# A decoder layer with sparse attention: subtractions shared out between VectorE and GpSimd, a written lookahead for each piece, and a new TensorE order

## The chip, the cores and the metric

The kernel runs on one core of a Trainium2 chip. The metric is the device time of one execution in microseconds. A core has TensorE (PE in the rows; its weight loads are PEld), VectorE (DVE), ScalarE (ACT), GpSimd (POOL) and SyncE (SP), which here only issues transfers. Each engine takes its instructions strictly in the order of its own queue.

## The reference

One layer over 512 positions of width 1024. The input is projected once; the columns go to three groups of mixers (causal pooling, a short gated convolution, and sparse attention with a compressed, a selected and a sliding branch), each with a SiLU gate; the groups' outputs are concatenated, projected, added to the scaled input and normalised.

```python
proj = x @ w_in
y_pool = jax.nn.silu(pool_z) * pool_mixer(pool_v, pool_w, pool_scale)
y_conv = jax.nn.silu(conv_z) * short_conv_mixer(conv_b, conv_c, conv_x, conv_w)
y_nsa = jax.nn.silu(nsa_z) * nsa_mixer(q, k_cmp, v_cmp, k_slc, v_slc, k_win, v_win, gates, ...)
y = jnp.concatenate([y_pool, y_conv, y_nsa], axis=-1) @ w_out
return layer_norm(ALPHA * x + y, ln_g, ln_b)
```

With 512 positions every block of keys is among the selected, so the selected and the sliding branch both attend to all earlier positions, with their own keys and values.

## The kernel before

**Split products.** TensorE multiplies in a rounded 32-bit form (fp32r). To keep precision, an operand is split into a rounded part and a rest: ScalarE writes the rounded part (`cast`, L79), and `rest` (L86) subtracts it from the original. A product then takes three matmuls. Line 86 is therefore one line for many subtractions: of weights (`hl<-raw,hl`, always on VectorE), of the turned attention weights (`ptl<-Y,pth`, always on GpSimd), of the gated outputs (`yln<-yo,yhn`) and others.

**Pieces and their order.** TensorE's instructions stand in the order in which the program writes them (`mm`, L67). The string `ORDER` (L26) writes it: each letter runs one step of a generator. `f` is the next piece of projection work: 12 matmuls with half of a chunk of 128 output columns, for which `weights` loads 256 KB, casts and subtracts; or a piece of the compression; or one of the eight first halves of the output projection. `s` scores a pair of heads against all keys of one branch (`scores`, L245): two matmuls into an `S` bank per head, VectorE adds the bias and takes the row's extreme (L257), ScalarE the exponential (L259). After that `scale` (L433) multiplies by the gate and the reciprocal of the sum (the gate product is L438, 128x2 or 128x4), and `turn` transposes through VectorE (L450) and a round trip to DRAM into `Y`. `v` (`values`, L459) splits `Y` into `pth` and `ptl` and multiplies with the values into an `O` bank. `c` scores the compressed keys (`cmp_scores`), `e` closes a query block of a head group (`finish`, L480): one matmul into its `O` bank, then for each of two halves a copy by ScalarE (L491) and an addition by VectorE (L492), then the product with the gate `zn` (L493) and the split. `o` is a piece of `second_part` (L644), which completes the output projection of 128 positions and normalises them.

**Banks.** Two `pj` banks take chunks, four `S` banks scores and small products, two `O` banks the attention outputs. A query block of a head group holds an `O` bank from its first `v` to the end of its `finish`; the blocks come in the order 3, 1, 0, 2 (`QB_ORDER`), first for one head group and then for the other. The third block therefore takes the bank of the first: its first `v` (the seventh of all) waits for the first `finish`.

**The other engines.** Their instructions are ordered by a planner, which simulates the engines and takes, among what is ready on an engine, the instruction with the highest priority. Earlier in the program is higher, and `tc.high_priority(offset=n)` moves what stands in it n places ahead. Before the change the offsets are one number per kind of work: weights 60 (`PRI_W`), compression 100 (`PRI_C`), normalisation 10 and 60 at the end, and 0 for scores, values, gates and finishes. The evacuation of the compression's input (`xs`, L332) and of queries has none. The planner's order is fixed when the program is built.

**The end.** `second_part` normalises each of four blocks: per half a sum of residual and product with its row sum (L664), a mean (L666), a square with its sum on ScalarE (L668), then small steps to the variance (L676 to L680), a power on GpSimd (L681), and two passes per half (L690, L696) before the store. The last block's second half is cut in two quarters.

Of the kernel before, what the change touches and what calls it, by code (L numbers as in the profile page):

```python
# [28 lines left out]
PRI_F = 0  # L29
# [23 lines left out]
def hybrid_layer(ctx, tc, xT, xres, wk4, wv, wc, wo, w1k, w1v, small, poolw, relb, onehot, lng, lnb,  # L53
# [266 lines left out]
    def blocks(i, pe_col):  # L320
        XS = y_tile("xs").rearrange("p a b -> p (a b)").rearrange("p (c t s) -> p c t s", c=16, t=2)
        pec = small_t[:, pe_col:pe_col + 16]
        act.activation(XS[:, :, 0, 31], pec, AF.Copy)
        rest(dve, XS[:, :, 1, 31], pec, XS[:, :, 0, 31])
        dve.memset(XS[:, :, :, 63].bitcast(F32), 0.0)
        p = yield from chunk(2 + i)
        for g in range(2):
            for par in range(2):
                src = p[64 * g:64 * g + 64]
                src = bass.AP(tensor=src.tensor, offset=src.offset + par, ap=[src.ap[0], [2, 16], [16, 31]])  # L330
                d = slice(64 * par, 64 * par + 64)
                act.activation(XS[d, :, 0, g * 32:g * 32 + 31], src, AF.Copy)  # L332
                rest(dve, XS[d, :, 1, g * 32:g * 32 + 31], src, XS[d, :, 0, g * 32:g * 32 + 31])
        return XS

    def compress(i, w1, w2_col):
# [9 lines left out]
        with tc.high_priority(offset=PRI_C):  # L346
            hs = tmp("hs", 256)
            act.activation(hs, hp[:, :256], AF.Copy)  # L348
        yield
        with tc.high_priority(offset=PRI_C):  # L350
# [12 lines left out]
        with tc.high_priority(offset=PRI_C):  # L363
# [18 lines left out]
    def gate_of(z, p):  # L382
        with tc.high_priority(offset=PRI_E):
            act.activation(z, p, AF.Tanh, scale=0.5)
            dve.scalar_tensor_tensor(z, z, 1.0, p, op0=OP.add, op1=OP.mult)  # L385
# [47 lines left out]
    def scale(qb, g, c, brs, P, st):  # L433
# [4 lines left out]
        dve.tensor_tensor(sv, sv, gv[:, :, 1 + brs[0]:1 + brs[0] + nb], op=OP.mult)  # L438
# [20 lines left out]
    def values(qb, g, c, brs, Y):  # L459
# [6 lines left out]
        for k0 in range(0, nk, 2):  # L466
# [6 lines left out]
            rest(pool, tl, t, th)  # L473
# [6 lines left out]
    def finish(qb, g, th):  # L480
# [6 lines left out]
        with tc.high_priority(offset=PRI_F):  # L487
# [31 lines left out]
    def put_y(k, y):  # L519
        y_parts()  # L520
        act.activation(ypc["h"][:, k], y, AF.Copy)
        rest(dve, ypc["l"][:, k], y, ypc["h"][:, k])
# [85 lines left out]
    def wo_parts(half, k):  # L608
        if (half, k) in WO:
            return WO[half, k]  # L610
        if k in (4, 5):
            with tc.high_priority(offset=PRI_W):
# [18 lines left out]
    def first_part(half, tb):  # L631
# [8 lines left out]
        dve.scalar_tensor_tensor(r, r, ALPHA, o, op0=OP.mult, op1=OP.add)  # L640

    GB = []

    def second_part(tb, final):  # L644
# [12 lines left out]
        for i, (half, a, b) in enumerate(cuts):  # L657
# [5 lines left out]
            with tc.high_priority(offset=PRI_END if final else PRI_LN):  # L663
                dve.scalar_tensor_tensor(x, x, 1.0, o, op0=OP.mult, op1=OP.add, accum_out=m[:, i:i + 1])  # L664
                if i == 0:
                    dve.tensor_scalar(m[:, 6:7], m[:, 0:1], -1.0 / 512 / 32, None, op0=OP.mult)  # L666

                act.activation(o, x, AF.Square, bias=m[:, 6:7], scale=1.0 / 32, accum_out=m[:, 3 + i:4 + i])  # L668
                if i == n - 2:
# [12 lines left out]
        on_pool = [] if tb in QB_ORDER[LN_POOL:] else [i for i in range(2) if LN_PAT[i] == "p"]  # L682
        for i, (half, a, b) in enumerate(cuts):
            x = R[tb, half][:, a:b]
            with tc.issue_after(ready.ins):
                if i in on_pool:
                    pool.tensor_scalar(x, x, m[:, 7:8], m[:, 11:12], op0=OP.add, op1=OP.mult)
                    pool.tensor_tensor(x, x, GB[half], op=OP.mult)
                else:
                    dve.scalar_tensor_tensor(x, x, m[:, 7:8], GB[half][:, a:b], op0=OP.add, op1=OP.mult)  # L690
        for i, (half, a, b) in enumerate(cuts):
            x = R[tb, half][:, a:b]
            if i in on_pool:
                pool.tensor_tensor(x, x, GB[2 + half], op=OP.add)
            else:
                dve.scalar_tensor_tensor(x, x, m[:, 11:12], GB[2 + half][:, a:b], op0=OP.mult, op1=OP.add)  # L696
            (nc.scalar if final and i == 1 else nc.sync).dma_start(out[tb, :, half, a:b], x)
# [15 lines left out]
    def q_chunk(c):  # L713
        p = yield from chunk(c - 2)
        queries(c, p)
# [32 lines left out]
    def attend():  # L748
        for n, u in enumerate(subs):
            with tc.high_priority(offset=PRI_A):  # L750
# [3 lines left out]
    def weigh():  # L754

        while scored:
            n, u, P, st = scored.pop(0)
            with tc.high_priority(offset=PRI_A):
                scale(*u, P, st)
                turned.append((u, turn(n, P)))  # L760

    def gather():
        while True:
            (qb, g, c, brs), Y = turned.pop(0)
            with tc.high_priority(offset=PRI_V):
# [104 lines left out]
```

## Time and profile before

| what | value |
|---|---|
| median of 3 runs | 275.31 us (274.36 to 276.69) |
| the profiled execution | 275.69 us, of which the span from first to last instruction 273.9 us |
| TensorE matmul busy | 251.7 us, 92% of the span |
| VectorE busy | 216.0 us, 79% |
| ScalarE busy | 185.3 us, 68% |
| GpSimd busy | 91.0 us, 33% |
| mean granted TensorE clock | 0.971 |

Matmuls overlap each other in the records, so a row's duration is longer than the pace: 24 matmuls of 128x512 advance the chain by 5.46 us. What tells whether TensorE is held is the idle time before a row (in brackets in the timeline) and the granted clock of a stretch, in which 1.00 is the upper of its two levels, 2.4 GHz, and 0.50 the lower, 1.2 GHz.

### The profile page before, as it was taken

To read this page: it belongs to the slowest core of one execution; us is meant where nothing else is said; L and a number is where in the kernel's file an instruction comes from. 1 tells how busy PE (TensorE), PEld (TensorE's weight loads), DVE (VectorE), ACT (ScalarE), POOL (GpSimd) and SP (SyncE) were. 2 spreads that over 40 slices of the span, in tenths; PEclk is the share of its full clock that TensorE was granted. 3 is DMA by queue.
4 is the path that set the end of the run, shared out by engine and by line. 5 is a ranking of instruction groups with operands and counts; after the bars stand their busy time and mean duration, and the time that the engine had idled before them with its cause. 6 is when DMAs were issued, how large, how long until landed. Compare 5 with 4: busy or idle time off the path is not lost.

```text
span 273.9 us, 4510 instructions
## 1 busy us (share of the span) xinstructions
PE 251.7 (92%) x1241; PEld 208.8 (76%) x1241; DVE 216.0 (79%) x568; ACT 185.3 (68%) x441; POOL 91.0 (33%) x112
## 2 busy tenths in 40 slices
PE   8899999969997899939999799999999999999970
PEld 5677997757887788738888678878888888888760
DVE  2672948757998999999897989899669648795685
ACT  3763748658998997877668999996586336452330
POOL 4100800040043345243337452355342153104831
PEclk9999999999999999968999889999999999999995
DMA  6864963783579787674566387798565897520232
GB/s 209 308 191 126 194 200 111 257 203 120 169 233 241 245 234 217 219 225 174 166 203 171 134 250 201 250 265 266 173 187 199 270 304 203 150 76 21 94 117 78
DMA packets 38454, 52.42 MB, mean 191 GB/s; under 512 B 4691, under 2 KB 22780, under 8 KB 38396
## 3 DMA queue, kind: packets, MB, share of 16 engines
q1 hardware_dynamic: 37964, 51.93, 62.4%
q8 instruction: 10, 0.16, 0.3%
q10 hardware_dynamic: 464, 0.20, 0.3%
q14 instruction: 16, 0.13, 0.2%
HBM read 38.47 MB, written 14.04 MB: 192 GB/s over the span
## 4 chain that ended last, share of the span: by engine, by line
PE 59%; DVE 13%; issue 10%; DMA 6%; POOL 5%; ACT 3%; SPq 2%; DVEq 0%; POOLq 0%; ACTq 0%
PE bk L69 48%; PE o L69 5%; PE s L69 4%; DVE hl L86 3%; POOL ptl L86 3%; DMA small_t<-small 2%; DVE P L257 2%; DMA scrp<-X 2%; DVE X L450 2%; DMA Y<-scrp 2%; DVE r L696 1%; ACT hl L79 1%; DVE r L664 1%; ACT bk L668 1%; POOL ln L681 1%
## 5 line engine op out<-in xcount | busy, mean ns | idle before, releaser
L69 PE MATMUL bk<-xh,hl 128*128 128x512 f32 x384 | 125.4, 396 | 3.0 <-DVE zn L385 2.2
L86 POOL TENSOR_TENSOR ptl<-Y,pth 128x512 fp32r<-128x512 f32 (+1 forms) x44 | 54.3, 1245 | 104.5 <-ACT pth L79 102.5
L69 PEld LDWEIGHTS bk<-xh,hl 128*128 128x128 f32 x384 | 72.6, 190 | 20.6 <-DVE zn L385 2.6
L69 PE MATMUL bk<-xl,hl 128*128 128x512 f32 x192 | 75.7, 394 | 0.0
L86 DVE TENSOR_TENSOR hl<-raw,hl 128x512 fp32r<-128x512 f32 (+1 forms) x72 | 51.2, 717 | 19.5 <-ACT hl L79 19.0
L79 ACT ACTIVATE hl<-raw 128x512 fp32r<-128x512 f32 (+1 forms) x72 | 42.9, 604 | 24.2 <-PE bk L69 19.9
L69 PEld LDWEIGHTS bk<-xl,hl 128*128 128x128 f32 x192 | 36.5, 190 | 7.3 <-DVE xl L86 0.3
L259 ACT ACTIVATE P<-P,st 128x512 f32<-128x512 f32 (+3 forms) x64 | 35.3, 553 | 4.0 <-DVE st L257 3.5
L441 ACT ACTIVATE P<-P,st 128x512 f32<-128x512 f32 (+3 forms) x64 | 31.1, 552 | 3.0 <-DVE st L438 2.4
L257 DVE CUSTOM_DVE_ANT_0 P<-s,T 128x512 f32<-128x512 f32 (+3 forms) x64 | 28.6, 482 | 1.7 <-PE s L69 1.2
L79 ACT ACTIVATE pth<-Y 128x512 fp32r<-128x512 f32 (+1 forms) x44 | 24.5, 582 | 6.6 <-POOL ptl L86 2.6
L450 DVE STREAM_TRANSPOSE X<-P 128x512 f32<-128x512 f32 (+2 forms) x48 | 27.7, 605 | 0.6 <-ACT P L441 0.3
L69 PE MATMUL o<-pth,VS 128*128 128x256 f32 x80 | 21.6, 297 | 4.8 <-DVE yo L492 4.7
L69 PE MATMUL s<-KS,qs 128*128 128x512 f32 (+2 forms) x96 | 23.8, 371 | 1.6 <-ACT hs L348 0.8
L69 PE MATMUL o<-ptl,VS 128*128 128x256 f32 x80 | 21.7, 299 | 3.2 <-POOL ptl L86 3.1
L69 PEld LDWEIGHTS s<-KS,qs 128*128 128x128 f32 x96 | 16.8, 194 | 5.0 <-ACT hs L348 1.1
L69 PEld LDWEIGHTS o<-pth,VS 128*128 128x128 f32 x80 | 15.9, 199 | 6.0 <-issue 5.1
L69 PE MATMUL bk<-hl,yhp 128*128 128x512 f32 x64 | 20.2, 396 | 0.0
L69 PEld LDWEIGHTS o<-ptl,VS 128*128 128x128 f32 x80 | 16.0, 200 | 5.1 <-POOL ptl L86 4.4
L668 ACT ACTIVATE bk<-r,ln 128x512 f32<-128x512 f32 (+1 forms) x9 | 5.8, 640 | 16.5 <-DVE ln L666 12.9
L69 PEld LDWEIGHTS bk<-hl,yhp 128*128 128x128 f32 x64 | 11.8, 188 | 2.6
L69 PE MATMUL bk<-hl,ylp 128*128 128x512 f32 x32 | 12.7, 395 | 0.0
(167 smaller groups left out, 376.5 us busy)
## 6 DMA issues: line engine op xcount, KB each, us to landing
raw<-wc SPq DMA_DIRECT2D x40, 256.0 KB, 3.2
scrp<-X SPq DMA_DIRECT2D x12, 512.0 KB, 3.1
Y<-scrp SPq DMA_DIRECT2D x48, 128.0 KB, 4.3
raw<-wo SPq DMA_DIRECT2D x16, 256.0 KB, 2.9
scrp<-X SPq DMA_DIRECT2D x8, 384.0 KB, 3.0
Y<-scrp SPq DMA_DIRECT2D x32, 96.0 KB, 2.4
r<-xres SPq DMA_DIRECT2D x8, 256.0 KB, 5.1
out<-r SPq DMA_DIRECT2D x7, 256.0 KB, 2.0
```

Source lines behind the costliest of these rows:

```text
L69: return tc.keep_in_program_order(pe.matmul(*args, **kw))
L79: act.activation(dst, src, AF.Copy)
L86: eng.tensor_tensor(dst, src, h.bitcast(F32), op=OP.subtract)
L257: dve.tensor_tensor_reduce(out=P[:, j, b], in0=p[:, b], in1=T[:, h, 512 - w:], scale=-1.0, scalar=BIG, op0=OP.add, op1=OP.min, accum_out=s ...
L259: act.activation(P[:, j, b], P[:, j, b], AF.Exp, bias=st[:, 0, j, b:b + 1], scale=-1.0, accum_out=st[:, 1, j, b:b + 1])
L441: act.activation(P[:, j, b], P[:, j, b], AF.Copy, scale=st[:, 1, j, b:b + 1])
L450: dve.transpose(X[:, :, :, h].rearrange("p j k s -> p k j s"), P[:, h].rearrange("p b (k j s) -> p (b k) j s", j=4, s=32))
L664: dve.scalar_tensor_tensor(x, x, 1.0, o, op0=OP.mult, op1=OP.add, accum_out=m[:, i:i + 1])
L668: act.activation(o, x, AF.Square, bias=m[:, 6:7], scale=1.0 / 32, accum_out=m[:, 3 + i:4 + i])
L681: pool.tensor_tensor(m[:, 11:12], m[:, 10:11], mhalf, op=OP.pow)
L696: dve.scalar_tensor_tensor(x, x, m[:, 11:12], GB[2 + half][:, a:b], op0=OP.mult, op1=OP.add)
```

## The change

Three things are rewritten; what is computed stays the same.

1. `ENG` gives each single subtraction or product its engine. Of the 68 weight subtractions that `weights` makes, 30 go to GpSimd; of the 44 `ptl` subtractions, 18 go to VectorE; of the 24 gate products of L438, 9 go to GpSimd; of the 8 products with `zn`, 4; of the 8 subtractions of `yln`, 1.
2. `AHEAD` gives each piece of each kind its own offset, 20 times a digit, in place of one offset per kind. Kinds that had none (compressed scores `k`, queries `q`, `xs` `x`, the splits of `put_y` `y`, the additions of `first_part` `r`) get one, and scaling (`m`) and turning (`t`) get one each.
3. `ORDER` is a new string with the same letters. The first `s` stands after 3 letters `f` instead of 8, the first `e` ahead of the twelfth `s` instead of behind it, the second `e` ahead of the seventh `v`; the sixth `c`, the ninth `v` and others move by up to three letters `f`.

At the end, the third block's normalisation passes are issued behind the last block's first mean; of the last block, the first of the second half's quarters may be normalised as soon as its mean is known, and the stores of the first half and of that quarter swap their queues.

```diff
-ORDER = 'ffffffffssfffffffffssfffsvfffssfvfffvfcsfsvfcfffsvsfffsevcsvevffffvscfevffsfsfsvcvsevffsfssvffcvsfvefffvffvsfsvfcefvffffvfvcffvfeffvefooooooooo'
+ORDER = 'fffsfffffsfffffffffssffsfvfffsfvsffsfvfcfsvfcfffsvsfffesvcsevvfffvfscfveffsfsfsvcvsevffcsfvssffvsffvefffvsfvfesvvfcffffvffcffevfffvfveooooooooo'
+AHEAD = {
+    'c': '959549', 'f': '41096608', 'k': '11011402', 'm': '421690533210053042023000', 'q': '20', 'r': '84751010',
+    's': '401032580053839606633100', 't': '002048505000085633022423', 'v': '091035350020997197125450',
+    'w': '006142361099275378536090313980932105459923933500690630432363221843055577',
+    'x': '43240150', 'y': '0505', 'z': '36060004',
+}
+ENG = {
+    'g': 'vpvpvpvvpvpvpvvvvvvpvpvp',
+    't': 'vvppppvppvppppvpppvvppppppvppvvpppvvvpvvvvpv',
+    'w': 'pvpvpvppppppvvpvpvvvvpppppvvvpvpvvvvvpppvvvvvvvvvpvpvvpvpvpvvvvvpppp',
+    'y': 'ppvpvvpv', 'z': 'vvvvpvvv',
+}
...
+    def ahead(kind):
+        i = cnt["+" + kind] = cnt.get("+" + kind, -1) + 1
+        return tc.high_priority(offset=20 * int(AHEAD[kind][i]))
+    def turn_of(kind):
+        i = cnt[kind] = cnt.get(kind, -1) + 1
+        return eng[ENG[kind][i]]
     def weights(src, n):
-        with tc.high_priority(offset=PRI_W):
+        with ahead("w"):
...
-            parts(raw, hl[:, 0, :n], hl[:, 1, :n])
+            parts(raw, hl[:, 0, :n], hl[:, 1, :n], turn_of("w"))
...
-        dve.tensor_tensor(sv, sv, gv[:, :, 1 + brs[0]:1 + brs[0] + nb], op=OP.mult)
+        turn_of("g").tensor_tensor(sv, sv, gv[:, :, 1 + brs[0]:1 + brs[0] + nb], op=OP.mult)
...
-            rest(pool, tl, t, th)
+            rest(turn_of("t"), tl, t, th)
...
-        with tc.high_priority(offset=PRI_F):
+        with ahead("f"):
...
+            while late:
+                with tc.issue_after(first.ins):
+                    late.pop()()
...
+                with tc.issue_after(early if final and i == 1 else ready.ins):
...
-            (nc.scalar if final and i == 1 else nc.sync).dma_start(out[tb, :, half, a:b], x)
+                (nc.scalar if final and i == 0 else nc.sync).dma_start(out[tb, :, half, a:b], x)
+        if tb == QB_ORDER[-2]:
+            late.append(norm)
+        else:
+            norm()
```

## Rows read from the trace of the kernel before

**Rows 1.** The head of the profile's page: the span, and busy time, share of the span and instructions of each engine; and the first line of the chain of waits that ended last, in shares of the span.

```profile
span 273.9 us, 4510 instructions
...
PE 251.7 (92%) x1241; PEld 208.8 (76%) x1241; DVE 216.0 (79%) x568; ACT 185.3 (68%) x441; POOL 91.0 (33%) x112
...
PE 59%; DVE 13%; issue 10%; DMA 6%; POOL 5%; ACT 3%; SPq 2%; DVEq 0%; POOLq 0%; ACTq 0%
```

**Rows 2.** The table of stretches: start and end of a stretch in us, its length, the busy time of each engine in it with the number of instructions, the granted TensorE clock, the DMA engines' busy share and GB/s.

```profile
42.00:64.00 22.00, 19.60 (x92) 15.80 (x91) 14.31 (x33) 14.52 (x33) 2.78 (x3) 1.00 0.61 180
...
64.00:182.00 118.00, 108.11 (x541) 90.76 (x540) 109.92 (x330) 104.42 (x275) 45.24 (x52) 0.96 0.69 207
...
182.00:230.00 48.00, 48.00 (x237) 40.50 (x236) 36.45 (x81) 27.45 (x59) 17.80 (x18) 1.00 0.74 229
...
265.60:273.90 8.30, 0.00 (x0) 0.00 (x0) 4.46 (x15) 1.79 (x6) 0.99 (x1) 0.66 0.27 97
```

**Rows 3.** The timeline of TensorE: four of its waits. Columns: start us, duration us, engine, line, operation, out<-in, shape, count, and in brackets the idle time before it and what ended it.

```profile
56.99 0.50 PE L69 MATMUL bk<-xh,hl 128*128 128x512 f32 x1 [2.17 <-DVE zn L385]
...
93.28 0.61 PE L69 MATMUL s<-KS,qs 128*128 128x384 f32 x2 [0.75 <-ACT hs L348]
...
120.56 0.55 PE L69 MATMUL o<-pth,VS 128*128 128x256 f32 x1 [4.73 <-DVE yo L492]
...
155.16 0.39 PE L69 MATMUL o<-ptl,VS 128*128 128x256 f32 x1 [1.32 <-POOL ptl L86]
```

**Rows 4.** The table of stretches again, by two microseconds, behind the two waits that lower the clock.

```profile
120.00:122.00 2.00, 1.44 (x6) 1.38 (x7) 1.91 (x8) 0.62 (x2) 0.00 (x0) 0.50 0.65 188
...
122.00:124.00 2.00, 2.00 (x8) 1.81 (x7) 1.88 (x8) 1.98 (x5) 0.38 (x1) 0.50 0.33 101
...
124.00:126.00 2.00, 2.00 (x8) 1.54 (x8) 1.91 (x8) 1.95 (x5) 1.67 (x2) 0.76 0.38 148
...
128.00:130.00 2.00, 2.00 (x11) 1.64 (x10) 1.93 (x6) 0.93 (x3) 0.20 (x1) 1.00 0.77 260
...
156.00:158.00 2.00, 2.00 (x6) 1.61 (x7) 1.94 (x7) 2.00 (x7) 0.99 (x1) 0.50 0.41 131
...
158.00:160.00 2.00, 1.86 (x10) 1.55 (x9) 2.00 (x13) 1.86 (x6) 1.54 (x2) 0.73 1.01 253
```

**Rows 5.** The timeline from the first `finish` to the end of the longest wait (the last matmul into its bank, the copy and the addition of either half, and one small product between them), and the same four steps of the last `finish`.

```profile
113.14 0.39 PE L69 MATMUL o<-pct,VC 128*128 128x512 f32 x1
...
115.14 0.38 ACT L491 ACTIVATE yo<-o 64x256 f32<-64x256 f32 x1
...
116.18 0.41 DVE L492 TENSOR_TENSOR yo<-o,yo 64x256 f32<-64x256 f32 x1
...
117.78 0.38 ACT L491 ACTIVATE yo<-o 64x256 f32<-64x256 f32 x1
...
118.67 1.21 DVE L554 TENSOR_TENSOR edge<-edge,pv 64x16 f32<-64x16 f32 x1
...
119.98 0.43 DVE L492 TENSOR_TENSOR yo<-o,yo 64x256 f32<-64x256 f32 x1
...
240.09 0.38 ACT L491 ACTIVATE yo<-o 64x256 f32<-64x256 f32 x1 [1.29 <-PE o L69]
...
242.22 0.43 DVE L492 TENSOR_TENSOR yo<-o,yo 64x256 f32<-64x256 f32 x1
```

**Rows 6.** Groups of VectorE instructions between 64 and 182 us: line, engine, operation, out<-in, shape, count, busy us in all, mean ns of one, idle time before them.

```profile
L86 DVE TENSOR_TENSOR hl<-raw,hl 128x512 fp32r<-128x512 f32 x31 | 22.7, 736 | 3.0 <-ACT hl L79 3.0
...
L438 DVE TENSOR_TENSOR st<-st,G 128x2 f32<-128x2 f32 (+1 forms) x19 | 4.8, 251 | 0.3
...
L493 DVE TENSOR_TENSOR yo<-yo,zn 128x256 f32<-128x256 f32 x4 | 1.8, 459 | 0.0
```

**Rows 7.** Groups of GpSimd instructions over the whole span, in the same columns.

```profile
L86 POOL TENSOR_TENSOR ptl<-Y,pth 128x512 fp32r<-128x512 f32 (+1 forms) x44 | 54.3, 1245 | 104.5 <-ACT pth L79 102.5
...
L681 POOL TENSOR_TENSOR ln<-ln,mhalf 128x1 f32<-128x1 f32 x4 | 4.0, 996 | 22.5 <-DVE ln L680 22.5
...
L86 POOL TENSOR_TENSOR bdl<-bd,bdh 128x256 fp32r<-128x256 f32 x1 | 0.7, 742 | 0.1
...
L418 POOL TENSOR_TENSOR pc<-pc,cm 128x124 f32<-128x124 f32 (+3 forms) x8 | 2.6, 331 | 6.8 <-DVE cm L417 3.0 <-DMA raw<-wc 1.5 <-ACT P L441 1.2
```

**Rows 8.** The timeline where a weight subtraction of VectorE meets a subtraction of GpSimd, and one that meets none.

```profile
106.15 1.28 POOL L86 TENSOR_TENSOR ptl<-Y,pth 128x512 fp32r<-128x512 f32 x1 [0.69 <-DMA raw<-wc]
...
106.27 1.71 DVE L86 TENSOR_TENSOR hl<-raw,hl 128x512 fp32r<-128x512 f32 x1
...
112.11 0.69 DVE L86 TENSOR_TENSOR hl<-raw,hl 128x512 fp32r<-128x512 f32 x1 [0.16 <-ACT hl L79]
```

**Rows 9.** The timeline of the end: the third block's normalisation, the last block's first cut between, and the last block's own normalisation.

```profile
261.74 1.41 DVE L690 SCALAR_TENSOR_TENSOR r<-r,ln,lng 128x512 f32<-128x512 f32 x2
...
263.73 0.68 DVE L664 SCALAR_TENSOR_TENSOR r<-r,bk 128x512 f32<-128x512 f32 x1
...
264.33 0.75 DVE L696 SCALAR_TENSOR_TENSOR r<-r,ln,lnb 128x512 f32<-128x512 f32 x1
...
265.34 0.15 DVE L666 TENSOR_SCALAR ln<-ln 128x1 f32<-128x1 f32 x1
...
267.64 0.16 DVE L680 TENSOR_TENSOR ln<-ln 128x1 f32<-128x1 f32 x1
```

More of the change, by code (lines that the diff above doesn't have):

```diff
@@ L331, in blocks @@
                 d = slice(64 * par, 64 * par + 64)
-                act.activation(XS[d, :, 0, g * 32:g * 32 + 31], src, AF.Copy)
-                rest(dve, XS[d, :, 1, g * 32:g * 32 + 31], src, XS[d, :, 0, g * 32:g * 32 + 31])
+                with ahead("x"):
+                    act.activation(XS[d, :, 0, g * 32:g * 32 + 31], src, AF.Copy)
+                    rest(dve, XS[d, :, 1, g * 32:g * 32 + 31], src, XS[d, :, 0, g * 32:g * 32 + 31])
         return XS
@@ L345, in compress @@
                 mm(hp[:, :256], x[:, c], hl[:, :, j * 128:j * 128 + 128], start=c == 0, stop=c == 15)
-        with tc.high_priority(offset=PRI_C):
+        with ahead("c"):
             hs = tmp("hs", 256)
@@ L349, in compress @@
         yield
-        with tc.high_priority(offset=PRI_C):
+        with ahead("c"):
             hq = bank("S", "hq")
@@ L362, in compress @@
         yield
-        with tc.high_priority(offset=PRI_C):
+        with ahead("c"):
             o = bank("S", "cmpo")
@@ L382, in gate_of @@
     def gate_of(z, p):
-        with tc.high_priority(offset=PRI_E):
+        with ahead("z"):
             act.activation(z, p, AF.Tanh, scale=0.5)
@@ L520, in put_y @@
         y_parts()
-        act.activation(ypc["h"][:, k], y, AF.Copy)
-        rest(dve, ypc["l"][:, k], y, ypc["h"][:, k])
+        with ahead("y"):
+            act.activation(ypc["h"][:, k], y, AF.Copy)
+            rest(dve, ypc["l"][:, k], y, ypc["h"][:, k])
     mix_z = {}
@@ L611, in wo_parts @@
         if k in (4, 5):
-            with tc.high_priority(offset=PRI_W):
+            with ahead("w"):
                 raw, _ = load(wo[k, half], 512)
@@ L639, in first_part @@
         r = R[tb, half]
-        dve.scalar_tensor_tensor(r, r, ALPHA, o, op0=OP.mult, op1=OP.add)
+        with ahead("r"):
+            dve.scalar_tensor_tensor(r, r, ALPHA, o, op0=OP.mult, op1=OP.add)
     GB = []
+    late = []
     def second_part(tb, final):
@@ L665, in second_part @@
                 if i == 0:
-                    dve.tensor_scalar(m[:, 6:7], m[:, 0:1], -1.0 / 512 / 32, None, op0=OP.mult)
+                    first = dve.tensor_scalar(m[:, 6:7], m[:, 0:1], -1.0 / 512 / 32, None, op0=OP.mult)
                 act.activation(o, x, AF.Square, bias=m[:, 6:7], scale=1.0 / 32, accum_out=m[:, 3 + i:4 + i])
@@ L714, in q_chunk @@
         p = yield from chunk(c - 2)
-        queries(c, p)
+        with ahead("q"):
+            queries(c, p)
     def pieces(fs):
@@ L749, in attend @@
         for n, u in enumerate(subs):
-            with tc.high_priority(offset=PRI_A):
+            with ahead("s"):
                 scored.append((n, u, *scores(*u)))
@@ L757, in weigh @@
             n, u, P, st = scored.pop(0)
-            with tc.high_priority(offset=PRI_A):
+            with ahead("m"):
                 scale(*u, P, st)
+            with ahead("t"):
                 turned.append((u, turn(n, P)))
@@ L764, in gather @@
             (qb, g, c, brs), Y = turned.pop(0)
-            with tc.high_priority(offset=PRI_V):
+            with ahead("v"):
                 values(qb, g, c, brs, Y)
@@ L775, in compressed @@
             assert pcts[0] - pcts[1] < len(PCT)
-            pcs[qb, g] = cmp_scores(qb, g)
+            with ahead("k"):
+                pcs[qb, g] = cmp_scores(qb, g)
             yield
```

60 lines of the change are left out of this document (34 added, 26 removed).

## The prediction

> **What bounds the kernel now.** I read the busy shares first, then the chain of waits. TensorE is busy for 92% of the span and holds 59% of the chain [rows 1], so the time is TensorE's work plus the time in which it is held or slowed. Next, the table of stretches says where it is held. Nothing is lost from 182 us on until its work ends: 48.0 of 48 us [rows 2]. The last 8.3 us hold no matmul, only the end of the normalisation. Between 64 and 182 us it is busy for 108.1 of 118 us, so 9.9 us are waits; between 42 and 64 it lacks 2.4 us [rows 2].
>
> In the same 118 us VectorE is busy for 109.9 and ScalarE for 104.4 us, GpSimd for 45.2 [rows 2]. The reader should see three engines near their limit there and one with room: VectorE has 8.1 us of idle time, and whatever TensorE waits for stands in a full queue.
>
> Then the timeline of TensorE, for what ended its waits. The longest is 4.73 us before the seventh `v`, ended by an addition of `finish` on VectorE; next come 2.17 us before a chunk (`zn` evacuated late), 1.32 us for a subtraction on GpSimd, 0.75 us for a bank [rows 3]. Last, the granted clock: behind the longest wait TensorE runs at the lower level, 0.50 from 120 to 124 us and 0.76 on average from 124 to 126, where the same two microseconds hold 8 matmuls and not 11 [rows 4]. What it lost there is busy time times the missing share of the clock: 1.44 x 0.50 + 2.0 x 0.50 + 2.0 x 0.24 = 2.2 us. Behind the 1.32 us it is 2.0 x 0.50 + 1.86 x 0.27 = 1.5 us [rows 4]. At full clock the stretch's matmuls need 108.1 - 3.7 = 104.4 us.
>
> **The shares of the engines.** All terms are for 64 to 182 us, since VectorE has room elsewhere. By the start times of the weight subtractions the 19th to 48th of the string fall there; 10 of them leave VectorE: 10 x 0.736 = 7.4 us [rows 6]. Of the 44 turned-weight subtractions [rows 7] the 3rd to 30th fall there, 28, and 7 of these arrive; one of this shape that meets nothing takes 0.69 us on VectorE [rows 8], so 4.8 us. Six gate products leave, 6 x 0.251 = 1.5, and three `zn` products, 3 x 0.459 = 1.4 us [rows 6]. VectorE: 7.4 + 1.5 + 1.4 - 4.8 = 5.5 us less, 104.4 in place of 109.9. GpSimd: 3 more long subtractions at 1.28 us [rows 8], three products of 256 columns at 0.74, and six tiny products that it never did before: the nearest rows are 0.33 us for a product of up to 124 columns and 1.0 us for a power of one column [rows 7]; I take 0.33, as the same operation, and keep 1.0 for the range. In all 3.8 + 2.2 + 2.0 = 8 us more (12 at the other end), 53 of 118: not a bound by its sum. These 5.5 us are no gain in themselves. They are room.
>
> A rule speaks against moving subtractions to GpSimd. A weight subtraction that starts beside one of GpSimd takes 1.71 us, one that meets none 0.69 [rows 8]. GpSimd's own takes 1.28. So the two take turns, and a piece that is moved costs almost twice as long and may hold up its old engine. The Trainium skill (GPSIMD Engine Reference, Specifications and Engine selection) says that GpSimd's SBUF interface is shared with VectorE, against instructions with two SBUF inputs, and that elementwise work belongs on VectorE since GpSimd is about twice as slow with two inputs; by that rule the moves lose. These rows agree with it for the single instruction. In the sum I take few collisions, for the 31 weight subtractions of the stretch now average 0.736 us beside 28 of GpSimd's [rows 6]: (0.736 - 0.69) x 31 = 1.4 us in all. The rest is a rival.
>
> **The longest wait.** The first `finish` issues its matmul at 113.14; its four steps start at 115.14, 116.18, 117.78 and 119.98 and end at 120.41, although they take only 0.38 + 0.41 + 0.38 + 0.43 = 1.6 us [rows 5]. Between them VectorE does scores and a 64x16 product that takes 1.21 us beside GpSimd. The last `finish`, among less work, needs 2.6 us from 240.09 to 242.65 [rows 5]. The change does two things to it. The first digit of `f` puts it 80 places ahead (0 before), and the matmul is issued ahead of the twelfth `s`. Until the seventh `v`, TensorE then has the 2.7 us that it has now (113.14 to 115.83), the twelfth `s` (four matmuls of 384 columns, 0.68 us at the pace of 0.2275 us for 512) and the second `e` (0.23): 3.6 us. The chain needs 0.39 for the matmul, 1.6 for the steps, and before each of four steps about half of a running 0.69 us instruction, 1.4: 3.4 us. It just fits; since the thirteenth `s` has a lead of 160 and can still push in, I keep 0.7 us. Gain 4.73 - 0.7 = 4.0 us (bounds 0 and 4.73). The 2.2 us of clock stand behind this wait and go with it (bounds 0 and 2.2). What is late next is the wait for `S` banks around it.
>
> **The chunk's wait.** At 56.99 TensorE has waited 2.17 us for a bank that `zn` or `xs` holds [rows 3]. GpSimd is busy 2.8 of the 22 us there [rows 2], and four of the six weight subtractions of these chunks go to it, 2.8 us off VectorE; `xs` gets leads of 20 to 80 places and `zn` 60. I take 1.4 us, two thirds, as the transfers of the turned weights crowd this stretch too; bounds 0 and 2.17.
>
> **The end.** The last block's first addition (L664) starts at 263.73, behind 1.41 us of the third block's passes from 261.74; its mean comes at 265.34 only, with another pass (0.75 us from 264.33) between [rows 9]. The change puts these passes behind that mean, and one quarter's pass into the wait before L680 at 267.64. VectorE's work in the last 10 us stays the same, and it is nearly full there, so only its small holes go: 0.5 us (bounds 0 and 1.0). The swapped store queues move one issue between two queues that both end with a store anyway; 0.
>
> **The rest.** The first `s` stands earlier: it only moves the two bias steps and exponentials of one score ahead of 42 us, where no wait is at stake; 0. The other waits of the stretch (9.9 - 4.73 = 5.2 us, with 1.5 us of clock) have no single cause that the change takes away: I leave them, bounds -4 and +6. Against that stand pieces that now come earlier, the ninth `v` by one `f` and the sixth `c` by three, and weights with a lead of 0: one new wait of the size of the present smaller ones, +1.0 us.
>
> **Sum.** The profiled execution took 275.69 us, 0.4 over the median of 275.31 and inside the runs' spread. -4.0 - 2.2 - 1.4 - 0.5 + 1.0 = -7.1, so 268.6; I say 268.5.
>
> **Rivals.** (1) The waits only move: the planner works from its own picture of the engines, and VectorE, ScalarE and TensorE all need 104.4 us of the 118, so what one piece gains by a lead another loses. For it: every offset is relative, and nearly all rise. Against it: one wait is worth 6.9 us with its clock, and its cover grows by arithmetic. New waits of 6 us eat the gain: 274.5. Chance 0.18.
>
> (2) Slower, by collisions: of the 31 long GpSimd subtractions then in the stretch (28 - 7 + 10) each may hold up a VectorE subtraction by 1.71 - 0.69 = 1.02 us. VectorE has 8.1 + 5.5 = 13.6 us of room, so from 13 collisions on it is the bound and TensorE waits for it at every bank. At 20 of 31 the cost is 20.4 - 13.6 = 6.8 us, with none of the gains: 282.5. Against it: the 1.4 us above is hardly two of 31 now. This is the outcome by the rule of the Trainium skill (GPSIMD Engine Reference, Specifications) on the shared interface. Chance 0.12.
>
> (3) More: the whole stretch falls near its floor, 104.4 + 3 us, 10.6 less, the chunk's wait goes wholly (2.2) and the end gives 0.5: 262.4. For it: GpSimd has half of its time free, and the longest wait's cover would do for smaller ones. Against it: three engines at 97% leave no room for jitter. Chance 0.15.
>
> **Numbers.** The forecast, from 264.5 to 272.6, has 0.55. About 1% (2.7 us) is what a measurement here can tell from no change. Faster by more: 0.55 + 0.15 = 0.70; within: 0.18; slower: 0.12. The range of 8 in 10 takes the forecast, two thirds of (3) and most of (1): 262.5 to 277.
>
> **What would show it.** Right: the wait before the seventh `v` under 1.5 us and a granted clock of 1.00 behind it; the chunk's wait under 1 us; VectorE near 104 us of work in that stretch; the first mean of the last block before 264.5 less the gain. Wrong: weight subtractions well above 0.74 us on VectorE, or new waits of TensorE for `ptl` or `hl` on GpSimd, above all with a clock of 0.50 behind them; a gain smaller than 3 us with the longest wait gone would make (1) true.

## The result, and the profile after

The changed kernel takes 273.45 us (median of 20 runs, 272.22 to 275.02) against 275.48 us for the kernel before beside it (20 runs); the ratio is 0.9926, 95% interval 0.9905 to 0.9946. It is faster by 2.0 us, not by 7. The profiled execution took 274.03 us with a span of 272.2 us, 1.7 us less than before. Lines of `kernel.py` are shifted: L86 is now L104, L69 L87, L385 L414, L438 L467, L491 L520, L492 L521, L556 L586; at the end L664 is now L696, L666 L698, L680 L717, L690 L729 and L696 L735. Versions with the old leads have two lines more (L586 is L588 there).

The head of the page, with the first line of the chain of waits, beside [rows 1]:

```profile
span 272.2 us, 4490 instructions
...
PE 250.7 (92%) x1241; PEld 208.4 (77%) x1241; DVE 203.6 (75%) x542; ACT 185.8 (68%) x441; POOL 114.0 (42%) x138
...
PE 64%; DVE 11%; issue 7%; ACT 6%; POOL 5%; DMA 3%; SPq 1%; POOLq 0%; DVEq 0%; ACTq 0%
```

The table of stretches, beside [rows 2]: TensorE is held as long as before in the stretch from 64 to 182 us (107.93 of 118 us busy, 108.11 before), though VectorE has become lighter there.

```profile
42.00:64.00 22.00, 20.43 (x95) 16.46 (x93) 13.89 (x30) 15.08 (x33) 4.99 (x6) 1.00 0.69 196
64.00:182.00 118.00, 107.93 (x541) 90.52 (x542) 104.72 (x322) 103.09 (x272) 55.87 (x67) 0.97 0.69 212
182.00:230.00 48.00, 48.00 (x235) 40.40 (x235) 35.86 (x76) 28.86 (x61) 17.15 (x15) 1.00 0.74 229
...
263.60:272.20 8.60, 0.00 (x0) 0.00 (x0) 5.29 (x17) 1.12 (x4) 0.99 (x1) 0.80 0.34 122
```

VectorE's 104.72 us and GpSimd's 55.87 us are near what the prediction gave (104.4 and 53). Two groups of VectorE there, beside [rows 6], and two of GpSimd:

```profile
L104 DVE TENSOR_TENSOR hl<-raw,hl 128x512 fp32r<-128x512 f32 x20 | 15.0, 748 | 0.8 <-ACT hl L97 0.8
L104 DVE TENSOR_TENSOR ptl<-Y,pth 128x512 fp32r<-128x512 f32 (+1 forms) x7 | 4.7, 682 | 0.0
```

```profile
L104 POOL TENSOR_TENSOR hl<-raw,hl 128x512 fp32r<-128x512 f32 x10 | 13.0, 1297 | 12.0 <-ACT hl L97 11.8 <-POOL st L467 0.2
...
L467 POOL TENSOR_TENSOR st<-st,G 128x2 f32<-128x2 f32 (+1 forms) x7 | 1.8, 262 | 7.3 <-DVE st L465 6.7 <-DVE pv L586 0.6
```

The mean weight subtraction on VectorE is 748 ns, hardly more than the 736 of before [rows 6]; the mean says nothing of what follows.

TensorE's waits after 54 us, those of 0.75 us and more and the smaller ones behind 146 us, beside [rows 3]:

```profile
55.29 0.50 PE L87 MATMUL bk<-xh,hl 128*128 128x512 f32 x1 [1.41 <-DVE zn L414]
...
91.19 0.62 PE L87 MATMUL s<-KS,qs 128*128 128x384 f32 x2 [1.20 <-ACT hs L377]
...
114.14 0.47 PE L87 MATMUL o<-pct,VC 128*128 128x512 f32 x1 [0.78 <-DMA pct<-scrc]
115.85 0.39 PE L87 MATMUL o<-pth,VS 128*128 128x256 f32 x1 [1.24 <-DVE yo L521]
...
123.76 0.50 PE L87 MATMUL bk<-ylp,bdh 128*128 128x512 f32 x1 [0.79 <-DVE ylp L104]
...
149.51 0.39 PE L87 MATMUL o<-ptl,VS 128*128 128x256 f32 x1 [1.36 <-POOL ptl L104]
...
150.65 0.39 PE L87 MATMUL o<-ptl,VS 128*128 128x256 f32 x1 [0.41 <-POOL ptl L104]
...
152.91 0.39 PE L87 MATMUL o<-ptl,VS 128*128 128x256 f32 x1 [0.62 <-POOL ptl L104]
...
154.15 0.38 PE L87 MATMUL o<-ptl,VS 128*128 128x256 f32 x1 [0.50 <-POOL ptl L104]
...
156.75 0.80 PE L87 MATMUL bk<-ylp,bdh 128*128 128x512 f32 x1 [1.76 <-DVE ylp L104]
```

**Where the gain went.** The eleventh `v` starts at 146.52, against 152.16 before: 5.6 us ahead. The first half chunk of the convolution, which stands behind the thirteenth `v` and a pooling product, ends at 163.07, against 164.25: 1.2 us ahead. So 4.5 us are lost in one stretch, 12.1 us long before and 16.55 after. Its rows, kernel before and after in this order, and four of two microseconds after the change:

```profile
152.00:164.30 12.30, 10.43 (x48) 8.34 (x47) 11.45 (x40) 11.53 (x33) 6.19 (x6) 0.86 0.67 200
```

```profile
146.50:163.10 16.60, 11.94 (x48) 9.07 (x46) 14.02 (x40) 14.27 (x38) 8.53 (x7) 0.79 0.58 185
...
156.00:158.00 2.00, 1.25 (x3) 1.06 (x4) 2.00 (x5) 2.00 (x7) 1.28 (x1) 0.52 0.49 145
158.00:160.00 2.00, 2.00 (x6) 1.52 (x6) 1.96 (x6) 1.98 (x5) 0.31 (x1) 0.50 0.64 200
160.00:162.00 2.00, 2.00 (x6) 1.56 (x5) 0.69 (x2) 1.98 (x7) 1.68 (x2) 0.50 0.46 184
162.00:164.00 2.00, 2.00 (x12) 1.77 (x11) 0.52 (x3) 1.10 (x3) 0.00 (x0) 0.77 0.93 262
```

Both hold the same 44 matmuls and the first four of the next piece. After the change they lose 1.25 x 0.48 + 2 x 0.50 + 2 x 0.50 + 2 x 0.23 = 3.1 us to the lower clock, which begins with the 1.76 us wait; before they lost 1.5 [rows 4]. The waits in it are 1.36 + 0.41 + 0.62 + 0.50 + 1.76 = 4.65 us against 1.8. Together 1.6 + 2.85 = 4.45: all of it. This is one execution's figure: the version with the old end (below), whose queues are the same here, takes 15.3 us for the stretch in its profile, so the loss is 3.2 to 4.5 us.

What the 1.76 us waited for is read from VectorE's timeline. First GpSimd in the same stretch, then VectorE after the change, then VectorE before:

```profile
147.84 2.75 POOL L104 TENSOR_TENSOR ptl<-Y,pth 128x512 fp32r<-128x512 f32 x2 [3.53 <-PE sc L87]
151.58 2.51 POOL L104 TENSOR_TENSOR ptl<-Y,pth 128x512 fp32r<-128x512 f32 x2 [0.99 <-ACT pth L97]
```

```profile
148.70 1.30 DVE L104 TENSOR_TENSOR hl<-raw,hl 128x512 fp32r<-128x512 f32 x1
...
151.68 1.21 DVE L586 COPY pv<-edge 64x16 f32<-64x16 f32 x1
...
156.02 0.68 DVE L104 TENSOR_TENSOR ylp<-pv,yhp 128x512 fp32r<-128x512 f32 x1
```

```profile
155.64 0.71 DVE L86 TENSOR_TENSOR hl<-raw,hl 128x512 fp32r<-128x512 f32 x1
...
156.74 0.17 DVE L556 COPY pv<-edge 64x16 f32<-64x16 f32 x1
...
160.04 0.69 DVE L86 TENSOR_TENSOR ylp<-pv,yhp 128x512 fp32r<-128x512 f32 x1
```

The weight subtraction now starts inside GpSimd's first `ptl`, takes 1.30 us instead of 0.71, and GpSimd's pair takes 2.75 us (2.27 before). The next `ptl` and the second edge copy of the pooling, a 64x16 copy of one input, now start within 0.1 us of each other: the copy takes 1.21 us instead of 0.17. It fills edge columns of the pooling mixer's result `pv`, and `ylp`, the rest of that result and an operand of the pooling product, is formed from `pv`. So `ylp` waits for the copy and starts 9.5 us behind the eleventh `v` and not 7.9. It is the place of the 1.32 us wait [rows 3], for which the prediction counted no change.

### The profile page after: what moved, and what is told of

Its sections match the earlier page's. It is cut to its first block, busy times and chain, and to the rows that moved or that the text cites. A ratio compares the mean times of both kernels' runs of the same rounds, so it can differ in the third digit from the quotient of the medians.

```text
span 272.2 us, 4490 instructions
## 1 busy us (share of the span) xinstructions
PE 250.7 (92%) x1241; PEld 208.4 (77%) x1241; DVE 203.6 (75%) x542; ACT 185.8 (68%) x441; POOL 114.0 (42%) x138
## 4 chain that ended last, share of the span: by engine, by line
PE 64%; DVE 11%; issue 7%; ACT 6%; POOL 5%; DMA 3%; SPq 1%; POOLq 0%; DVEq 0%; ACTq 0%
PE bk L87 53%; PE o L87 5%; PE s L87 4%; DMA X<-xT 2%; DVE X L479 2%; POOL hl L104 2%; ACT P L287 2%; DVE P L285 2%; ACT P L470 1%; DVE hl L104 1%; DMA Y<-scrp 1%; POOL ln L718 1%; ACT hl L97 1%; PE sc L87 1%; ACT pth L97 1%
## 5 line engine op out<-in xcount | busy, mean ns | idle before, releaser
L87 PE MATMUL bk<-xh,hl 128*128 128x512 f32 x384 | 126.5, 400 | 1.9 <-DVE zn L414 1.4
L87 PEld LDWEIGHTS bk<-xh,hl 128*128 128x128 f32 x384 | 73.4, 192 | 19.0 <-DVE zn L414 1.8
L87 PE MATMUL bk<-xl,hl 128*128 128x512 f32 x192 | 76.2, 397 | 0.0
L104 POOL TENSOR_TENSOR hl<-raw,hl 128x512 fp32r<-128x512 f32 (+1 forms) x30 | 37.0, 1238 | 44.2 <-ACT hl L97 36.7
L104 POOL TENSOR_TENSOR ptl<-Y,pth 128x512 fp32r<-128x512 f32 (+1 forms) x26 | 33.7, 1307 | 32.1 <-ACT pth L97 25.9
L87 PEld LDWEIGHTS bk<-xl,hl 128*128 128x128 f32 x192 | 36.9, 192 | 7.5 <-DVE xl L104 0.3
L104 DVE TENSOR_TENSOR hl<-raw,hl 128x512 fp32r<-128x512 f32 (+1 forms) x42 | 30.4, 727 | 7.2 <-ACT hl L97 6.2
L87 PE MATMUL s<-KS,qs 128*128 128x512 f32 (+2 forms) x96 | 22.9, 360 | 1.8 <-ACT hs L377 1.2
L87 PE MATMUL o<-ptl,VS 128*128 128x256 f32 x80 | 20.6, 289 | 3.4 <-POOL ptl L104 3.4
L87 PE MATMUL o<-pth,VS 128*128 128x256 f32 x80 | 20.3, 283 | 1.3 <-DVE yo L521 1.2
L87 PE MATMUL bk<-hl,yhp 128*128 128x512 f32 x64 | 20.2, 396 | 0.0
L87 PEld LDWEIGHTS s<-KS,qs 128*128 128x128 f32 x96 | 16.1, 188 | 4.5 <-ACT hs L377 1.5
L87 PEld LDWEIGHTS o<-ptl,VS 128*128 128x128 f32 x80 | 15.1, 188 | 5.2 <-POOL ptl L104 4.5
L87 PEld LDWEIGHTS o<-pth,VS 128*128 128x128 f32 x80 | 15.1, 188 | 2.3 <-DVE yo L521 1.6
L104 DVE TENSOR_TENSOR ptl<-Y,pth 128x512 fp32r<-128x512 f32 (+1 forms) x18 | 12.2, 695 | 2.1 <-PE bk L87 1.3
```

Of the source, the lines that this page charges most:

```text
L87: return tc.keep_in_program_order(pe.matmul(*args, **kw))
L104: eng.tensor_tensor(dst, src, h.bitcast(F32), op=OP.subtract)
```

## The experiments

All times stand beside runs of the kernel before on the same chip; their medians were 275.24 to 276.02 us.

**1. Which part gives what.** The change has four parts that can be put back alone: the shares, the leads, the TensorE order and the end. Old shares, everything else new:

```diff
-ENG = {'g': 'vpvpvpvvpv...', 't': 'vvppppvv...', 'w': 'pvpvpvpp...', 'y': 'ppvpvvpv', 'z': 'vvvvpvvv'}
+ENG = {'g': 24 * 'v', 't': 44 * 'p', 'w': 68 * 'v', 'y': 8 * 'v', 'z': 8 * 'v'}
```

> The changed kernel with all subtractions and products back on their old engines; leads, TensorE order and end stay new. Theory 1 (the waits only move: TensorE, VectorE and ScalarE are all near full from 64 to 182 us, so each part alone shifts waits about): within 1% of the kernel before, 272.7 to 278.2 us, with the longest wait at the seventh v short but other waits long. Theory 2 (the shares carry the gain, as VectorE gets room): 1% or more above the changed kernel, 276 us and more, VectorE busy again over 214 us. Theory 3 (the new shares cost, by collisions of GpSimd and VectorE around the jam at 146 to 164 us, and order and leads carry the gain): faster than the changed kernel, 268 to 271 us.

Only the shares (old leads, TensorE order and end):

```diff
-AHEAD = {'c': '959549', 'f': '41096608', ...}
+AHEAD = {'c': 6 * '5', 'w': 72 * '3', 'f': 8 * '0', 's': 24 * '0', ...}
-ORDER = 'fffsfffffsfffffffffss...'
+ORDER = 'ffffffffssfffffffffss...'
...
-            late.append(norm)
+            norm()
```

> The kernel before with only the new shares. Theory 1: 273 to 278 us. Theory 2: 272 to 274 us, as fast as the changed kernel. Theory 3: slower than before, 277 us and more, with the wait at the seventh v still over 4 us.

The old TensorE order, everything else new:

```diff
-ORDER = 'fffsfffffsfffffffffss...'
+ORDER = 'ffffffffssfffffffffss...'
```

> The changed kernel with the old TensorE order. If the order carries the gain at the seventh v (the prediction's cover of 3.6 us instead of 2.7): the wait there is again over 3 us, with a granted clock of 0.50 behind it, and the time is 275 us or more. If the lead alone carries it: the wait is 1 to 3 us, without low clock. Theory 1 lets the total be within 1% of before either way.

The old leads, everything else new (kinds that had no offset before have none, the others 0):

```diff
-AHEAD = {'c': '959549', 'f': '41096608', ...}
+AHEAD = {'c': 6 * '5', 'w': 72 * '3', 'f': 8 * '0', 's': 24 * '0', ...}
```

> The changed kernel with the old leads (60 for weights, 100 for the compression, none elsewhere). If the lead of finish carries the gain at the seventh v: the wait there is over 3 us, time 275 us or more. If the order alone does: under 2.5 us. Theory 1: total 272 to 278 us.

The old end, everything else new:

```diff
-                with tc.issue_after(early if final and i == 1 else ready.ins):
+                with tc.issue_after(ready.ins):
...
-            late.append(norm)
+            norm()
```

> The changed kernel with the end of the kernel before: the third block's passes without the wait for the last block's mean, the second half's first quarter normalised after the variance, the stores' queues as before. The prediction's term (the new end gains 0.5 us): 0.5 us slower than the changed kernel, about 274. The trace's reading (from TensorE's last matmul to the end of the span 8.35 us before, 8.6 after): 0.2 to 0.5 us faster, about 273.

The kernel before with only the new TensorE order, and with only the new leads:

```diff
-ORDER = 'ffffffffssfffffffffss...'
+ORDER = 'fffsfffffsfffffffffss...'
```

> The kernel before with only the new TensorE order (old shares, old leads, old end). If the order by itself shortens the wait at the seventh v: that wait is under 3 us and the time under 274. If the three parts only work as a set (old shares in the changed kernel made it 284.6 us, the old order 280.2, the new shares alone 275.0): 275 to 280 us.

```diff
-AHEAD = {'c': 6 * '5', 'w': 72 * '3', 'f': 8 * '0', 's': 24 * '0', ...}
+AHEAD = {'c': '959549', 'f': '41096608', ...}
```

> The kernel before with nothing but the new leads (old shares, old TensorE order, old end). Theory (a lead sets only where a piece lands in a queue, and these were found for the other shares and order; with the old shares VectorE has no room to take a piece that lands badly): slower, 280 to 293, with the stretch from the eleventh v to the next half chunk above 15 us. Rival (leads on their own hardly matter): 275 to 276.

Measured:

| shares | order | leads | end | median us | ratio to before, 95% interval | eleventh `v` to end of the half chunk, us |
|---|---|---|---|---|---|---|
| old | old | old | old | 275.48 | 1 | 12.1 |
| new | old | old | old | 274.97 | 0.9983, 0.9952 to 1.0014 | 12.1 |
| old | new | old | old | 274.75 | 0.9978, 0.9944 to 1.0013 | 12.1 |
| old | old | new | old | 279.13 | 1.0119, 1.0076 to 1.0162 | 15.3 |
| new | new | old | new | 275.67 | 1.001, 0.9983 to 1.0037 | 12.1 |
| new | old | new | new | 280.24 | 1.0178, 1.0145 to 1.0212 | 15.3 |
| old | new | new | new | 284.58 | 1.0362, 1.0326 to 1.0397 | 17.6 |
| new | new | new | old | 273.19 | 0.9922, 0.9891 to 0.9952 | 15.3 |
| new | new | new | new | 273.45 | 0.9926, 0.9905 to 0.9946 | 16.55 |

Shares and order are worth nothing alone, nor together without the new leads. The end is worth nothing. The leads alone cost 3 us, and gain only on top of both other parts. The last column tells where they cost: every version with the new leads has the lengthened stretch, none with the old.

Not all came as expected. With the old shares VectorE is busy for 221.1 us and 284.58 us is far above the kernel before, as if the shares carried the gain; but then the shares alone should have given 272 to 274. With the order alone the wait before the seventh `v` stays at 3.69 us and the time is just under the 275 to 280 of its second case; with the old order that wait is 2.57 us with a granted clock of 0.89 from 110 to 126 us, between the two cases. The leads alone stay just short of 280.

**2. One lead.** In the changed kernel the 44th weight piece goes from 60 places ahead to 40. On VectorE that weight subtraction and the instruction that makes `zn` (L414) change places, on ScalarE a cast and the step that evacuates `zn`, on SyncE a few transfers; TensorE's and GpSimd's queues stay as they are.

```diff
-    'w': '006142361099275378536090313980932105459923933500690630432363221843055577',
+    'w': '006142361099275378536090313980932105459923923500690630432363221843055577',
```

> The changed kernel with one digit changed: the lead of the 44th weight piece from 60 to 40 places. VectorE's order differs in one spot only: that piece's subtraction and zn's product change places around the bias steps of the 17th s, ahead of the edge copies of the second pooling mixer; TensorE's and GpSimd's orders are the same. Theory J (a jam: the gain of 6.7 us that the changed kernel has by 123 us is lost between the 11th v and the first half of conv_c, which take 16.6 us in it and 12.1 in the kernel before, because that subtraction meets a turned-weight subtraction of GpSimd, which ends 0.45 us later, so that an edge copy of 16 columns waits 1.05 us for the next one): these pieces take 12 to 13 us again, and the time is 268.5 to 270.5 us. Theory 1 (the waits only move): what is won there is lost at the next full stretch, 272 us and more.

Measured: 269.86 us (269.17 to 270.77), ratio 0.9804, 0.9759 to 0.985. The stretch is 12.1 us again and the wait for `ylp` 0.34 us. Its row, TensorE's row, and VectorE in it:

```profile
146.80:158.90 12.10, 10.37 (x48) 7.98 (x46) 11.37 (x39) 11.48 (x32) 6.34 (x6) 0.86 0.69 199
```

```profile
155.43 0.50 PE L87 MATMUL bk<-ylp,bdh 128*128 128x512 f32 x1 [0.34 <-DVE ylp L104]
```

```profile
150.29 0.71 DVE L104 TENSOR_TENSOR hl<-raw,hl 128x512 fp32r<-128x512 f32 x1
...
151.39 0.17 DVE L586 COPY pv<-edge 64x16 f32<-64x16 f32 x1
...
154.69 0.69 DVE L104 TENSOR_TENSOR ylp<-pv,yhp 128x512 fp32r<-128x512 f32 x1
```

The subtraction stands behind three scores, where GpSimd is nearly done with its pair, and both stalls are gone. The stretch gives 3.2 to 4.5 us, the time 3.6, as the theory had it. This version is faster than both kernels.

**3. The same lead the other way.** In the version with all old leads (275.67 us, 12.1 us in the stretch) only this lead is raised, from 60 to 100 places.

```diff
-    'w': '333333333333333333333333333333333333333333333333333333333333333333333333',
+    'w': '333333333333333333333333333333333333333333353333333333333333333333333333',
```

> New shares, new TensorE order and new end with the old leads, as in the run with the old leads (275.67 us), but the 44th weight piece gets a lead of 100 places instead of 60. In the program's queues only this differs: on VectorE that weight subtraction and the zn product change places, so that the subtraction again stands two scores behind the pooling product; one ScalarE cast, some transfers. Theory (the one lead puts the subtraction beside a subtraction of GpSimd, and the hold-up runs on): the subtraction takes 1.2 to 1.7 us in place of 0.71, a 64x16 edge copy about 1.2 in place of 0.17, the stretch from the eleventh v to the end of the next half chunk is 15 to 17 us in place of 12.1, and the time is 278.5 to 280. Rival (the new leads as a whole make the jam; lowering this lead cured it only beside them): 275.0 to 276.4, with the stretch at 12.1 us.

Measured: 279.05 us (276.61 to 280.24), ratio 1.0104, 1.006 to 1.0147. That is 3.4 us more than the version without it (2.6 by the two ratios, since they ran on different chips), and the stretch is 15.3 us. VectorE in it, then TensorE:

```profile
155.57 1.30 DVE L104 TENSOR_TENSOR hl<-raw,hl 128x512 fp32r<-128x512 f32 x1
...
158.54 1.22 DVE L588 COPY pv<-edge 64x16 f32<-64x16 f32 x1
...
162.89 0.69 DVE L104 TENSOR_TENSOR ylp<-pv,yhp 128x512 fp32r<-128x512 f32 x1
```

```profile
163.63 0.50 PE L87 MATMUL bk<-ylp,bdh 128*128 128x512 f32 x1 [1.74 <-DVE ylp L104]
```

The same rows come back, to 0.02 us, and `ylp` again starts 9.5 us behind the eleventh `v` (153.38). The 3 us that the leads cost alone are as much as the 3.2 us of this one place, where that version has the same two rows (1.30 and 1.22 us). With only one of the two other parts they cost more: 5.3 us on the new shares, where the old order has two further waits, 1.78 and 1.21 us, for `ptl` subtractions that now stand on VectorE; and about 10 on the new order, which was not taken apart.

**4. Only the second stall.** In the changed kernel the two edge copies of each pooling mix go to ScalarE; the weight subtraction stays where it collides.

```diff
-            dve.tensor_copy(v[r, 16:32], e[r])
+            act.activation(v[r, 16:32], e[r], AF.Copy)
```

> The changed kernel with the pooling mixers' edge copies (64x16) on ScalarE in place of VectorE; the weight subtraction stays where it meets GpSimd's. Theory J, if the blocked copy is what costs: the wait before the second pool_out (1.76 us) goes under 0.7 and the low clock behind it with it, 269.5 to 272 us. If the delayed turned weights cost and not the copy: waits at the 12th and 13th v stay at 2.9 us in all and the time stays at 273 us or more.

Measured: 271.37 us (270.75 to 272.6), ratio 0.9861, 0.9814 to 0.9909. Here the subtraction still takes 1.34 us, the copy 0.21 us on ScalarE:

```profile
149.97 1.34 DVE L104 TENSOR_TENSOR hl<-raw,hl 128x512 fp32r<-128x512 f32 x1
```

```profile
151.41 0.21 ACT L586 ACTIVATE pv<-edge 64x16 f32<-64x16 f32 x1
```

The stretch is 12.3 us (eleventh `v` at 147.78, half chunk's end at 160.11). So it is the held copy, ahead of `ylp`, that made the long wait and its clock; the held subtraction alone is absorbed. The version with the old shares is the reverse case: there the subtraction ahead of the copy meets nothing (0.69 us), the copy alone is held (1.21 us), and the wait for `ylp` is 1.75 us. The time gains 2.1 us, not all of 3.6; the rest was not traced.

**5. Cover for the first `finish`.** Two waits are left ahead of the seventh `v`, 0.78 and 1.24 us. On the version with one lead changed, one `f` is moved up from behind the eighth `v`, once behind the second `e`, once ahead of it:

```diff
-ORDER = '...fffesvcsevvfffvfscfv...'
+ORDER = '...fffesvcsefvvffvfscfv...'
```

> The changed kernel with the 44th weight piece's lead at 40 (269.86 us), and one f moved in ORDER from behind the eighth v to a place between the second e and the seventh v. Theory (the first finish takes some 5.8 us from its matmul to its last addition because its four steps queue behind other work on ScalarE and VectorE, so only more TensorE work in between covers it): the wait of 1.23 us before the seventh v goes, and with it the lower clock behind it; the 0.78 us before the second e stay: 267.0 to 268.2. Rival (the waits only move: the half chunk waits for its weights or its bank, or the finish ends later by the same amount): 269.5 to 270.5.

```diff
-ORDER = '...fffesvcsevvfffvfscfv...'
+ORDER = '...fffesvcsfevvffvfscfv...'
```

> As the run before in this list, but the f stands ahead of the second e, so that it covers the wait for the transfer of the turned compressed weights too. Theory (cover): both waits go, 0.78 + 1.23 us and the lower clock behind them: 266.2 to 267.5. Rival (the waits only move): 269.5 to 270.5, since the second finish now ends later and the eighth-to-tenth v or a chunk waits in its place.

Measured: 274.6 us (ratio 0.9947, 0.9924 to 0.9971) and 273.59 us (0.991, 0.9877 to 0.9943). Both are slower than the 269.86 us that they start from; the rival did better, though even it did not expect a loss. In the first version the wait before the seventh `v` is gone, and TensorE waits 1.76 and 2.40 us at the first pooling product. In the second version the waits before the second `e` and the seventh `v` are gone, and TensorE waits instead at the same product, which had no wait:

```profile
122.24 0.80 PE L87 MATMUL bk<-yhp,bdh 128*128 128x512 f32 x1 [2.24 <-ACT yhp L590]
...
125.04 0.80 PE L87 MATMUL bk<-ylp,bdh 128*128 128x512 f32 x1 [2.00 <-DVE ylp L104]
```

It came to that product 3.9 us earlier than in the version with one lead changed (120.00 against 123.94 us), while `ylp` came later (124.29 us, against 122.83) since a weight subtraction (0.69 us) now stands ahead of it on VectorE and a pooling product there was held by GpSimd (1.22 us for 0.75). The waits moved, and doubled from 2.0 to 4.2 us.

## Why the prediction was wrong

The likeliest case, 264.5 to 272.6 us, was wrong and rival (1), "the waits only move", came true, also by its own sign (a gain under 3 us with the longest wait gone): 274.5 against 273.45 measured, inside the range of 262.5 to 277. Its mechanism was not the one given there: three engines near their limit were not what ate the gain, but one place in the queues, by collisions of the kind that rival (2) priced at 1.02 us.

- **The shares: right.** VectorE lost 5.2 us of work in the stretch, for 5.5 predicted, GpSimd gained 10.6 for 8. The tiny products cost 0.26 us on GpSimd, for 0.33 taken; seven came and not six. That this is room and no gain was right too: the shares alone are worth nothing.
- **The longest wait: right direction, mis-sized.** 4.73 us became 0.78 + 1.24 = 2.0 us, a gain of 2.7 for the 4.0 of the sum. The cover was nearly as reckoned, 3.84 us of TensorE's work for 3.6. But the chain of the first `finish` took 5.8 us from its matmul to the end of its last addition, 3.4 in the prediction. Half a running instruction ahead of each step was too little: its rows, beside [rows 5], show gaps of 0.95, 1.19, 0.67 and 1.01 us, in which ScalarE and VectorE work through others. One reason given was void: with the first digit of `f` at 0 in place of 4 the built program of the changed kernel is the same, instruction by instruction. No part did it alone: the wait is 3.69 us with the order, 3.58 with the leads, 0.99 + 2.29 with shares and order.

```profile
109.99 0.39 PE L87 MATMUL o<-pct,VC 128*128 128x512 f32 x1
...
111.33 0.38 ACT L520 ACTIVATE yo<-o 64x256 f32<-64x256 f32 x1
...
112.90 0.41 DVE L521 TENSOR_TENSOR yo<-o,yo 64x256 f32<-64x256 f32 x1
...
113.98 0.38 ACT L520 ACTIVATE yo<-o 64x256 f32<-64x256 f32 x1
...
115.37 0.43 DVE L521 TENSOR_TENSOR yo<-o,yo 64x256 f32<-64x256 f32 x1
```

- **Its clock: gone in this profile, but worth less.** The granted clock from 110 to 126 us is 1.00 after and 0.79 before. It is 0.89 with the old end and with one lead changed, although the two waits ahead of the seventh `v` are the same there to 0.05 us; so the 2.2 us are not sure to go with a wait of this size. Nor are they all gain: from the seventh `v` to the eleventh TensorE takes 30.7 us after and 31.6 before, and 31.1 and 31.2 in those two versions. At full clock it comes to the first pooling product sooner and waits 0.79 us there for `ylp` (123.76 above), a wait that the two versions don't have. Its row after the change and with the old end:

```profile
110.00:126.00 16.00, 13.19 (x69) 10.60 (x68) 15.13 (x45) 13.68 (x33) 8.93 (x11) 1.00 0.71 227
```

```profile
110.00:126.00 16.00, 13.98 (x64) 11.46 (x64) 15.19 (x45) 13.51 (x33) 8.16 (x9) 0.89 0.64 202
```

- **The chunk's wait: mis-sized.** 2.17 became 1.41 us, a gain of 0.76 for 1.4. The room that the shares make does it only with the old order: there the wait is 0.74 us with the new shares and leads, and 1.47 with the leads alone. With the new order the shares change nothing (2.17 us with the order alone, 2.22 with shares and order), and the leads bring it to 1.41.
- **The end: wrong, by 0.7.** From TensorE's last matmul to the span's end it is 8.6 us for 8.35 before. The first mean comes earlier, as predicted, but the third block's second passes (1.41 us from 263.34) now hold the last cut's addition:

```profile
261.61 0.15 DVE L698 TENSOR_SCALAR ln<-ln 128x1 f32<-128x1 f32 x1
...
263.34 1.41 DVE L735 SCALAR_TENSOR_TENSOR r<-r,ln,lnb 128x512 f32<-128x512 f32 x2
264.67 0.41 DVE L696 SCALAR_TENSOR_TENSOR r<-r,bk 128x256 f32<-128x256 f32 x1
...
266.23 0.16 DVE L717 TENSOR_TENSOR ln<-ln 128x1 f32<-128x1 f32 x1
```

- **The rest: the step that failed.** It took the other waits as they were and put "one new wait of the size of the present smaller ones, +1.0 us". Up to the eleventh `v` that held: one came, of 0.79 us, and the other small ones together are 0.8 us shorter. Then came 3.2 to 4.5 us in one stretch (3.6 in the time, by the version with one lead changed), at the place of the 1.32 us wait with its clock [rows 3, 4], which was known and counted with no change. The bounds of -4 and +6 held it; the value did not. What the step missed is that a lead does not only advance a piece; it sets what GpSimd is doing when the piece starts, and that the cheap instruction behind it (0.17 us) can be the one on the path. The prediction had such a row before it, a 64x16 product of 1.21 us beside GpSimd [rows 5], but priced weight subtractions alone. The sum of collisions was no guide: two of them, 0.6 and 1.05 us, in a chain with a low-clock stretch behind it cost 3.6 us.

By the rows the kernel is 4.7 us ahead at the seventh `v`; 4.3 of these are waits, 2.7 for the longest, 0.8 for the chunk's and 0.8 for smaller ones. At the eleventh it is 5.6 us ahead. +4.5 in the stretch, -0.8 behind it (1.96 us ahead at TensorE's end against 1.2) and +0.25 at the end leave 1.7, the difference of the spans. Without the collisions the time is 269.86 us, within the forecast and near its 268.5. That nearness is partly luck: the longest wait, the chunk's, the clock and the end each gave less than their terms, and gains that the sum left out made up for part of it.

## What to carry to other kernels

When work is moved between VectorE and GpSimd, don't price collisions by a mean over the stretch: go through the queue of the piece that releases the next matmul, and look at what GpSimd runs when each two-input instruction and each copy ahead of it starts. When a many-knob change gains less than its parts promise, find the stretch where the lead over the old trace is lost, and undo the smallest knob that reorders it; here one number of 220 was worth more than the whole change. Covering a wait can bring out a later one that it was hiding, so look at what TensorE needs next before moving work ahead of it.

## What the runs showed of the hardware

A 64x16 copy with one input on VectorE, 0.17 us by itself, takes 1.21 us when it starts just behind a GpSimd subtraction of 128x512, and ends with that subtraction: 151.68 + 1.21 = 152.89, 151.58 + 1.28 [rows 8] = 152.86. The Trainium skill (SBUF — State Buffer, SBUF: two separate sides) says that VectorE and GpSimd share one port pair as an exclusive lock, which whichever starts first holds for its whole instruction, and that VectorE asks for it with two SBUF inputs or in a two-port performance mode; the same section counts an fp32 copy from SBUF to SBUF among the latter. The trace agrees on both: the copy, which started 0.1 us behind the subtraction, ended only with it. The prediction, which looked at two-input instructions alone, had not thought of the copy. Scores beside the same subtractions were not held: 0.41 us, as elsewhere. The other side is held too: GpSimd's pair of subtractions took 2.75 us beside the colliding one of VectorE and 2.32 in the version with one lead changed, where that starts later. ScalarE does the same copy in 0.21 us while GpSimd subtracts.
